# HGRN2 within-chunk products: one 64-wide block as two 32-wide ones, and another order of the small products

## The chip, the cores and the metric

The kernel runs on one core of a Trainium2 chip. A run is told by its device time in microseconds. The kernel before was run three times: 2319.0, 2328.68 and 2331.19 us, median 2328.68 us. Its profile is of one more execution, of 2322.79 us.

TensorE (PE in the profile) multiplies; VectorE (DVE), ScalarE (ACT) and GpSimd (POOL) work element by element; SyncE (SP) issues the DMAs.

## The reference, cut to what matters

One layer with two branches: a gated DeltaNet and an HGRN2 recurrence, over 256 context tokens and 2048 latent tokens in both directions. The change lies in the HGRN2 branch. With k = 1 - f and g = log f, the state of one head obeys

```python
# S_t = diag(f_t) S_{t-1} + k_t v_t^T ,  o_t = S_t^T q_t ; 4 heads, dk = dv = 128
qg, kg = q * exp(G), k * exp(-G)          # G: running sum of g in a chunk
attn = where(incl, einsum('bhncd,bhnsd->bhncs', qg, kg), 0.0)
o_c = einsum('bhcd,bhdv->bhcv', qg_c, S) + einsum('bhcs,bhsv->bhcv', attn_c, v_c)
S = S * gl_c[..., None] + einsum('bhcd,bhcv->bhdv', kd_c, v_c)
```

`attn` is a lower triangle (an upper one for the reversed direction): token c sees token s only from its own past. All arrays are float32.

## The kernel before, in words

The tokens are projected first, then comes the HGRN2 stage (lines 483 to 674), then the DeltaNet stages, then the merge of the branches. In the HGRN2 stage the kernel takes chunks of 128 tokens, four chunks (index `i`) to a scan group of 512 tokens. `scan_group(h, d, g, ps, S)` does one group of head `h` and direction `d`; latent groups (`lat`) are those with outputs: 4 heads, 2 directions and 4 groups make 32 of them. A group has these steps: ACT and DVE turn the projected gate into decays (lines 502 to 561), DVE and POOL make the scaled copies `ag`, `bg`, `a64`, `b64`, `b32`, PE transposes (L577) and forms the state update `pS` (L582), PE forms the triangle `pat`, DVE copies its valid part to `atB` (L604), and PE adds the state's part and the triangle's part into `pw` (L612, L613) while DVE carries the state on (L618).

The triangle of one 128-token chunk is built of blocks, because the decays of far tokens need a scale of their own: four diagonal blocks of 32 by 32 (the loop before line 600), then two blocks of 32 by 32 that join the 32-token blocks in pairs, and one of 64 by 64 that joins the two halves. All contract over the 128 partitions. `mm` (L591) issues each of them: L593 in direction 0, L595 in direction 1. Where its output lies in `pat` decides which 32-column strips of the PE array hold its weights: an output on partitions 32k to 32k+31 uses strip k, the 64 by 64 block uses strips 0 and 1 (direction 0) or 2 and 3 (direction 1). The two joining blocks of 32 use strips 0 and 2 (direction 0) or 1 and 3 (direction 1). The four diagonal blocks use strips 0, 1, 2, 3. A float32 product is two passes on PE, each with a weight load (LDWEIGHTS, on the line PEld) and a MATMUL.

`proj` (L205 to L207), called by `head_units` and `gate_block`, fills PE between the groups' steps with full-width products of the next head. What stands in which order on PE is not the order of the source: `TileContext(nc, schedule_with_timeline_sim=True)` (L1184) has a planner at build time that simulates the engines and puts the instructions of each engine into one fixed order. So full-width products (L577, L582, L612, L613, L205 to L207) can stand between two products of one group's triangle.

Of the kernel before, what the change touches and what calls it, by code (L numbers as in the profile page):

```python
# [39 lines left out]
def block_kernel(ctx, tc, x, c, ctx_in, c_ctx, w_mod, b_mod, w_in, conv_w, a_log, dt_bias,  # L40
# [436 lines left out]
    with tc.tile_pool(name="rb", reuse_waits="tile", bufs=1, side="right") as rb, \  # L477
# [12 lines left out]
        def bl(a):  # L490
            return slice(32 * a, 32 * a + 32)

        def b4(t):
            return t.rearrange("p c (b t) -> p c b t", t=32)

        def scan_group(h, d, g, ps, S):
# [56 lines left out]
            a = X.rearrange("p (c t) -> p c t", t=P)  # L553
# [9 lines left out]
            def fb(f, m):  # L563
                return f.unsqueeze(3).to_broadcast([P, k_, m, 32])
# [18 lines left out]
            if lat:  # L583
                a64 = rb.tile([P, 4, 64], F32, tag="a64", name="a64")
                b64 = rb.tile([P, 4, 64], F32, tag="b64", name="b64")
                b32 = rb.tile([P, 4, 64], F32, tag="b32", name="b32")
                ve.tensor_tensor(out=b4(a64), in0=b4(a)[:, :, 2:4], in1=fb(f2, 2), op=ALU.mult)
                po.tensor_tensor(out=b4(b64), in0=b4(b)[:, :, 0:2], in1=fb(f3, 2), op=ALU.mult)
                po.tensor_tensor(out=b4(b32), in0=b4(b)[:, :, 0:4:2], in1=fb(f4, 2), op=ALU.mult)

                def mm(i, am, bm, asl, bsl):  # L591
                    if d == 0:
                        te.matmul(out=pat[bsl, i, asl], lhsT=bm, rhs=am, start=True, stop=True)  # L593
                    else:
                        te.matmul(out=pat[asl, i, bsl], lhsT=am, rhs=bm, start=True, stop=True)  # L595

                for i in range(4):
                    for k in range(4):
                        mm(i, a[:, i, bl(k)], b[:, i, bl(k)], bl(k), bl(k))
                for i in range(4):  # L600
                    for k in range(2):
                        mm(i, a[:, i, bl(2 * k + 1)], b32[:, i, bl(k)], bl(2 * k + 1), bl(2 * k))
                    mm(i, a64[:, i, :], b64[:, i, :], slice(64, 128), slice(0, 64))
                ve.copy_predicated(out=atB[d], mask=mk[d].unsqueeze(1).to_broadcast([P, 4, P]), data=pat)  # L604
                o = rb.tile([P, 4, P], F32, tag="o", name="o")
                if d == 1:
                    sy.dma_start(out=o, in_=oP[h, g])
                pw = pb.tile([P, 4, P], F32, tag="o", name="pw")
                qg = ag if d == 0 else bg
# [54 lines left out]
        for h in range(H):  # L664
            fill = head_units(h + 1) if h + 1 < H else gate_units(NEARLY + GA)
            for d in range(2):
                w = load_w((C_FF, C_FB)[d] + h * P)
                S = None
                for j, g in enumerate(((4, 0, 1, 2, 3), (4, 3, 2, 1, 0))[d]):
                    S = scan_group(h, d, g, proj(w, g), S)  # L670
                    for _ in range(FBI[d][j] if h + 1 < H else FB[j] * d):
                        next(fill, None)
            for _ in fill:
                pass
# [514 lines left out]
```

## Time and profile before

| | us |
|---|---|
| runs before, median (lowest to highest) | 2328.68 (2319.0 to 2331.19) |
| the profiled execution | 2322.79 |
| its span in the trace | 2321.1 |
| PE busy | 2210.0 (95%) |
| DVE busy | 1401.9 (60%) |
| ACT busy | 907.8 (39%) |
| POOL busy | 756.9 (33%) |

The span runs from the first to the last instruction of the program; 1.7 us of the execution lie around it. Busy time is the time in which an engine has at least one instruction in work; PE's instructions overlap, so that one that the profile shows as 0.2 us long may start a few nanoseconds behind the one ahead of it. The mean granted clock of PE was 0.982 of full speed. The HGRN2 triangle's products run between 524.8 and 1060.6 us.

### The profile page before, as it was taken

The page shows a single profiled execution, that of the slowest core. Times are in us where ns is not written, and L with a number is a line of the kernel's source. Part 1 is how long each engine was busy: PE and PEld are TensorE (multiplying, and loading weights), DVE is VectorE, ACT ScalarE, POOL GpSimd, SP SyncE. Part 2 cuts the span into 40 slices and gives each one's busy share as a digit, 9 for nine tenths or more (in the row PEclk, how much of TensorE's full clock was granted, in tenths as well). Part 3 has the DMA queues.
Part 4 walks back from the last instruction along what each step waited for, and adds up shares of the span by engine and source line. Part 5 has one row for each costly group of instructions (what it writes and reads, how often), then busy time and mean ns, then how long its engine had stood idle before and what let it go on. Part 6 is the DMA issues. An engine that isn't in the chain of part 4 may idle for free. (4 is left out here: it accounts for less than half of the span.)

```text
span 2321.1 us, 39923 instructions
## 1 busy us (share of the span) xinstructions
PE 2210.0 (95%) x14998; PEld 1848.3 (80%) x14998; DVE 1401.9 (60%) x3184; ACT 907.8 (39%) x2298; POOL 756.9 (33%) x736
## 2 busy tenths in 40 slices
PE   7899999999999999999989999999989889999998
PEld 2778888888888888888878778788878878878887
DVE  5926666636766667774374877872332358566655
ACT  3523222234343444432434445544544454344321
POOL 3613343302221122224534445311133234334341
PEclk8999999999999999999999999999999999999999
DMA  8312222322322322224656588786887855434322
GB/s 317 112 36 73 66 73 71 87 63 78 92 71 85 91 74 87 85 76 132 178 163 195 185 243 256 206 240 204 250 271 264 264 192 166 127 110 128 118 82 78
DMA packets 298329, 330.24 MB, mean 142 GB/s; under 512 B 77536, under 2 KB 216918, under 8 KB 298136
## 3 DMA queue, kind: packets, MB, share of 16 engines
q1 hardware_dynamic: 298135, 327.69, 45.9%
q8 instruction: 118, 1.93, 0.4%
q14 instruction: 76, 0.61, 0.1%
HBM read 216.83 MB, written 110.79 MB: 141 GB/s over the span
## 5 line engine op out<-in xcount | busy, mean ns | idle before, releaser
L205 PE MATMUL ps<-uhi,wh 128*128 128x512 f32 (+1 forms) x1824 | 707.9, 388 | 5.4 <-DVE uhi L293 2.6
L206 PE MATMUL ps<-ulo,wh 128*128 128x512 f32 (+1 forms) x1824 | 705.8, 387 | 3.0 <-DVE ulo L295 2.7
L207 PE MATMUL ps<-uhi,wl 128*128 128x512 f32 (+1 forms) x1824 | 706.2, 387 | 0.5 <-POOL wl L197 0.5
L205 PEld LDWEIGHTS ps<-uhi,wh 128*128 128x128 f32 x1824 | 345.6, 190 | 71.0 <-DVE uhi L293 3.9
L206 PEld LDWEIGHTS ps<-ulo,wh 128*128 128x128 f32 x1824 | 345.7, 190 | 66.8 <-DVE ulo L295 3.9
L207 PEld LDWEIGHTS ps<-uhi,wl 128*128 128x128 f32 x1824 | 345.2, 189 | 64.5 <-POOL wl L197 1.3
L197 POOL TENSOR_TENSOR wl<-ws,wh 128x512 fp32r<-128x512 f32 x144 | 192.2, 1335 | 536.7 <-ACT wh L196 512.3
L196 ACT CAST wh<-ws 128x512 fp32r<-128x512 f32 x144 | 89.5, 621 | 288.5 <-DMA ws<-in_w_in_dram 192.3
L1089 PE MATMUL py<-yh,wab 128*128 128x256 f32 x512 | 151.4, 296 | 26.5 <-DVE mg L1092 25.6
L393 DVE SCALAR_TENSOR_TENSOR acc<-raw,cols,acc 128x512 f32<-128x512 f32 x192 | 153.9, 855 | 0.8
L1090 PE MATMUL py<-yl,wab 128*128 128x256 f32 x512 | 148.3, 290 | 2.6 <-POOL yl L1073 2.6
L1091 PE MATMUL py<-yh,wab 128*128 128x256 f32 x512 | 147.9, 289 | 0.0
L1089 PEld LDWEIGHTS py<-yh,wab 128*128 128x128 f32 x512 | 100.7, 197 | 31.0 <-DVE mg L1092 29.0
L572 POOL TENSOR_TENSOR bg<-s,fz 128x512 f32<-128x512 f32 (+1 forms) x36 | 38.0, 1057 | 263.5 <-ACT X L552 96.9
L1109 PE MATMUL pso<-uhi,mh 128*128 128x512 f32 x256 | 102.9, 404 | 3.6 <-ACT mh L1095 2.3
L1090 PEld LDWEIGHTS py<-yl,wab 128*128 128x128 f32 x512 | 101.0, 197 | 3.8 <-POOL yl L1073 3.2
L1111 PE MATMUL pso<-uhi,ml 128*128 128x512 f32 x256 | 102.0, 404 | 2.0 <-DVE ml L1096 1.9
L1110 PE MATMUL pso<-ulo,mh 128*128 128x512 f32 x256 | 101.6, 399 | 0.0
L1091 PEld LDWEIGHTS py<-yh,wab 128*128 128x128 f32 x512 | 101.2, 198 | 0.0
L1073 POOL TENSOR_TENSOR yl<-gt,yh 128x512 fp32r<-128x512 f32 x32 | 46.7, 1478 | 165.2 <-ACT yh L1072 165.2
L1096 DVE TENSOR_TENSOR ml<-mg,mh 128x256 fp32r<-128x256 f32 x64 | 53.0, 832 | 70.1 <-ACT mh L1095 69.4
L1095 ACT CAST mh<-mg 128x256 fp32r<-128x256 f32 x64 | 41.2, 651 | 135.7 <-DVE mg L1093 135.4
(371 smaller groups left out, 4135.8 us busy)
## 6 DMA issues: line engine op xcount, KB each, us to landing
ws<-in_w_in_dram SPq DMA_DIRECT2D x144, 256.0 KB, 3.2
gT<-gt SPq DMA_DIRECT2D x96, 256.0 KB, 3.2
kv<-knvD SPq DMA_DIRECT2D x36, 512.0 KB, 5.4
kq<-qkvD SPq DMA_DIRECT2D x32, 512.0 KB, 5.5
an<-atN SPq DMA_DIRECT2D x32, 512.0 KB, 5.7
mg<-gT SPq DMA_DIRECT2D x64, 256.0 KB, 3.6
qkvD<-acc SPq DMA_DIRECT2D x48, 256.0 KB, 2.3
l<-qkvD SPq DMA_DIRECT2D x16, 768.0 KB, 5.1
```

The lines of the kernel that those rows point to most:

```text
L196: ac.copy(out=wh[:, j:j + 4, :], in_=ws)
L197: po.tensor_tensor(out=wl[:, j:j + 4, :], in0=ws, in1=wh[:, j:j + 4, :].bitcast(F32), op=ALU.subtract)
L205: te.matmul(out=ps, lhsT=wh[:, k, :], rhs=uhi[gi][:, k, :], start=(k == 0), stop=False)
L206: te.matmul(out=ps, lhsT=wh[:, k, :], rhs=ulo[gi][:, k, :], start=False, stop=False)
L207: te.matmul(out=ps, lhsT=wl[:, k, :], rhs=uhi[gi][:, k, :], start=False, stop=(k == KB - 1))
L393: ve.scalar_tensor_tensor(out=a_, in0=raw[:, o + k:o + k + n], scalar=wk, in1=a_, op0=ALU.mult, op1=ALU.add)
L1089: te.matmul(out=py[:, i, :], lhsT=wh[:, k, ms_], rhs=yh[i][:, k, :], start=(k == 0), stop=False)
L1090: te.matmul(out=py[:, i, :], lhsT=wh[:, k, ms_], rhs=yl[i][:, k, :], start=False, stop=False)
L1091: te.matmul(out=py[:, i, :], lhsT=wl[:, k, ms_], rhs=yh[i][:, k, :], start=False, stop=(k == H - 1))
L1109: te.matmul(out=ps, lhsT=mh[:, k, ts_], rhs=wout[0][k][:, ns], start=(k == 0), stop=False)
L1110: te.matmul(out=ps, lhsT=mh[:, k, ts_], rhs=wout[1][k][:, ns], start=False, stop=False)
L1111: te.matmul(out=ps, lhsT=ml[:, k, ts_], rhs=wout[0][k][:, ns], start=False, stop=(k == KB - 1))
```

## The change

The 64 by 64 block of each chunk becomes two products of 32 weight columns and 64 streamed columns: in direction 0 the weights are 32 columns of `b64` and all of `a64` is streamed, in direction 1 the weights are 32 columns of `a64` and all of `b64` is streamed. The same numbers land on the same partitions of `pat`. In each chunk the four products are issued with the strips 0, 2, 0, 1 in direction 0 and 3, 1, 3, 2 in direction 1, where it was strips 0, 2, (0 and 1) and 1, 3, (2 and 3). The diagonal blocks are as before.

```diff
+                def across32(i, k):
+                    mm(i, a[:, i, bl(2 * k + 1)], b32[:, i, bl(k)], bl(2 * k + 1), bl(2 * k))
+
+                def across64(i, k):
+                    if d == 0:
+                        mm(i, a64[:, i, :], b64[:, i, bl(k)], slice(64, 128), bl(k))
+                    else:
+                        mm(i, a64[:, i, bl(k)], b64[:, i, :], bl(2 + k), slice(0, 64))
+
                 for i in range(4):
                     for k in range(4):
                         mm(i, a[:, i, bl(k)], b[:, i, bl(k)], bl(k), bl(k))
                 for i in range(4):
-                    for k in range(2):
-                        mm(i, a[:, i, bl(2 * k + 1)], b32[:, i, bl(k)], bl(2 * k + 1), bl(2 * k))
-                    mm(i, a64[:, i, :], b64[:, i, :], slice(64, 128), slice(0, 64))
+                    across32(i, d)
+                    across32(i, 1 - d)
+                    across64(i, d)
+                    across64(i, 1 - d)
```

## Rows read from the trace of the kernel before

**Rows 1.** The page: busy time by engine, and the PE line of 40 slices.
```profile
PE 2210.0 (95%) x14998; PEld 1848.3 (80%) x14998; DVE 1401.9 (60%) x3184; ACT 907.8 (39%) x2298; POOL 756.9 (33%) x736
...
PE   7899999999999999999989999999989889999998
```
**Rows 2.** Windows: start:end, length, each engine's busy time, clock, DMA.
```profile
520.00:1065.00 545.00, 544.01 (x4402) 455.40 (x4401) 383.96 (x1046) 219.11 (x400) 126.67 (x129) 1.00 0.28 83
520.00:965.00 445.00, 444.62 (x3504) 373.63 (x3503) 306.62 (x835) 179.88 (x328) 99.57 (x102) 1.00 0.28 83
965.00:1018.00 53.00, 53.00 (x475) 44.11 (x473) 45.14 (x129) 23.53 (x44) 13.36 (x15) 1.00 0.25 73
```
**Rows 3.** Waits of PE, 520 to 1065 us: total us, times, longest.
```profile
PE pS L582 <- DMA v<-vB: 0.6, 1, 0.6
PE pw L612 <- DVE S L618: 0.4, 1, 0.4
```
**Rows 4.** Timeline of PE, one group's joining blocks: start, us to last end, count.
```profile
526.25 0.26 PE L593 MATMUL pat<-X,b 128*32 128x32 f32 x4
526.44 0.33 PE L593 MATMUL pat<-a,b 128*64 128x64 f32 x2
526.70 0.26 PE L593 MATMUL pat<-X,b 128*32 128x32 f32 x4
...
527.77 0.33 PE L593 MATMUL pat<-a,b 128*64 128x64 f32 x2
528.02 0.49 PE L612 MATMUL pw<-S,ag 128*128 128x128 f32 x2
```
**Rows 5.** Timeline of PE, diagonal blocks on four strips, two stretches.
```profile
524.83 0.33 PE L593 MATMUL pat<-X,s 128*32 128x32 f32 x16
...
591.27 0.41 PE L595 MATMUL pat<-s,X 128*32 128x32 f32 x26
591.50 0.20 PE L595 MATMUL pat<-b,X 128*32 128x32 f32 x1
591.51 0.20 PE L595 MATMUL pat<-s,X 128*32 128x32 f32 x2
591.53 0.25 PE L595 MATMUL pat<-b,X 128*32 128x32 f32 x3
591.71 0.33 PE L595 MATMUL pat<-b,a 128*64 128x64 f32 x2
```
**Rows 6.** Tile pat: count, ns of one (min/median/max), first and last start.
```profile
L593 PE MATMUL pat<-X,b x256: 196/196/217, 526.3 to 1001.0; 128*32 128x32 f32 x128
L593 PE MATMUL pat<-a,b x128: 222/246/271, 526.4 to 1001.2; 128*64 128x64 f32 x128
L595 PE MATMUL pat<-b,X x256: 196/196/217, 591.5 to 1060.3; 128*32 128x32 f32 x128
L595 PE MATMUL pat<-b,a x128: 222/246/270, 591.7 to 1060.6; 128*64 128x64 f32 x128
```
**Rows 7.** Timeline of PE, joining blocks with full-width products among them.
```profile
548.34 0.33 PE L593 MATMUL pat<-a,b 128*64 128x64 f32 x2
548.60 0.49 PE L612 MATMUL pw<-S,ag 128*128 128x128 f32 x2
548.92 0.39 PE L613 MATMUL pw<-v,atB 128*128 128x128 f32 x2
549.24 0.26 PE L593 MATMUL pat<-X,b 128*32 128x32 f32 x4
...
1058.48 0.33 PE L595 MATMUL pat<-b,a 128*64 128x64 f32 x2
...
1060.01 0.33 PE L595 MATMUL pat<-b,a 128*64 128x64 f32 x2
...
1060.45 0.33 PE L595 MATMUL pat<-b,a 128*64 128x64 f32 x2
```
**Rows 8.** Waits of DVE, 520 to 1065 us: total us, times, longest.
```profile
DVE atB L604 <- PE pat L595: 31.8, 9, 4.9
```
**Rows 9.** Groups by line and shape: count, busy us, mean ns of one, idle before.
```profile
L613 PE MATMUL pw<-v,atB 128*128 128x128 f32 x256 | 49.5, 275 | 0.0
```

## The prediction, made blind

> **What bounds the kernel now.** I read the page first: PE is busy 95% of the span, and in no slice under seven tenths [rows 1]. Then the windows over the stretch in which the changed products run, 520 to 1065 us: PE is busy for 544.0 of 545 us, DVE for 384.0, ACT for 219.1, POOL for 126.7, the DMAs have 28%, and the clock is granted whole [rows 2]. Then PE's own waits there: 0.6 and 0.4 us, and nothing else [rows 3]. So in this stage PE's sequence is the time: a nanosecond taken out of it comes off the end, until some other engine is late. The chain that ended last shows only the end of the kernel and says nothing here.
>
> Being busy isn't the same as being used well. The timeline of one group's joining blocks shows the cost [rows 4]: four passes of the 32-wide blocks open at 526.25, the two passes of the 64-wide one at 526.44, the next 32-wide ones at 526.70, and the fourth turn ends where the full-width L612 opens, at 528.02. That is 1.77 us for four turns, 443 ns a turn, for eight array passes that stream 32 or 64 columns.
>
> **The prices.** In the diagonal blocks, on four strips in rotation, 16 passes end 0.33 us after the first began and 26 passes 0.41 us [rows 5]: ten passes more in 0.08 us, 8 ns a pass, so 32 ns a pass on any one of four strips. I take 31 to 32. A pass is 196 ns long in the records at 32 streamed columns and 222 at 64 [rows 6]; the 26 ns between them are 32 columns more, so a 64-column pass occupies a strip for about 57 ns if nothing else holds it.
>
> Between strips there is no pause: in the second stretch of rows 5 a joining product (`b,X`) starts at 591.50, before the last two diagonal passes (`s,X`) at 591.51. The strips go their own way, past each other in program order. Between widths there is one. In rows 4 the last of four 32-wide passes starts 0.26 - 0.196 = 0.06 us after the first, at 526.31, and the 64-wide one opens at 526.44: 0.13 us later, where 32-wide ones follow in 8 to 32 ns. Its second pass starts 0.33 - 0.222 = 0.11 us on, at 526.55, and the next 32-wide one at 526.70: 0.15 us. Of that a 64-column pass itself takes 53 (twice 26), a 32-column one 26, so both ways about 0.1 us passes with the array empty. Each 64-wide block costs two such pauses, or about 200 of the 443 ns.
>
> **The change part by part.** (1) The 64-wide form goes: 256 passes, 128 products [rows 6]. In their place stand 256 products of 32 weight columns and 64 streamed ones, 512 passes, so MATMUL and LDWEIGHTS grow by 256 each, to 15254 [rows 1].
>
> (2) All products of a triangle now have one width, so the pauses inside it go. The new turn, in direction 0, is strip 0 with 32 columns, strip 2 with 32, strip 0 with 64, strip 1 with 64; in direction 1 it is 3, 1, 3, 2. The fullest strip has 2 x 31 + 2 x 57 = 176 ns of passes, the others 114 and 62, beside it. From below a turn takes 176 ns. From above, if a strip's second product must wait for the whole turn ahead of it and nothing runs beside anything: 4 x 31 + 4 x 57 = 352 ns. In between, if the two products ahead must end before the two behind start: about 234 (62 + 114 and two fillings of about 29). I take 176, because rows 5 show the strips passing each other, and a strip that never runs dry sets the pace.
>
> (3) The number of turns. Followed along the timeline, of 128 64-wide blocks 87 are followed by another 32-wide product (the first at 526.44, the last at 1058.48), 39 by a full-width product (527.77 the first, 1060.45 the last), and two more have a full-width one ahead of them (one at 1060.01) [rows 4, 7]. That is 32 group ends and some places where the planner put a full-width product in. For the 87: 443 - 176 = 267 ns each, 23.2 us. For the 39 the pause to full width stays: first product 0 to about 53 ns with its weight load, then 31 + 57, and 152 to the full-width product, 293 ns for 443, so 150 ns each, 5.8 us. The two I count like the 39: 0.3 us. Sum: 29.3 us, in 32 groups 0.9 us each.
>
> The same counts with a turn of 234: 18.2 + 5.8 - 2.3 (the pair takes 58 ns longer in the 39 as well) = about 21.7 us. With 352: 87 x 91 = 7.9, nothing at the 39 (352 - 57 + 152 = 447), 8 us.
>
> (4) What else moves. No wait is new: the same copies `a64`, `b64`, `b32` feed the same products, and the order within a turn asks for none sooner than before. No DMA, no buffer, no DVE instruction is added. The copy to `atB` waits for PE, not PE for it: DVE stood 31.8 us in nine such waits [rows 8], and it moves up with PE.
>
> (5) What is late next. A group that is 0.9 us shorter on PE meets producers that aren't. PE waited 0.4 us for the state on DVE once [rows 3]; were that so in each of 32 groups, 13 us would be lost, from below none. DVE has 30% to spare over the stage, but it is 85% busy from 965 to 1018 us, where four groups stand close [rows 2]: 11.3 of 13.25 us a group, so 0.9 us less leaves it room there too. Rows 3 stand nearer to the lower end; I take 5 us.
>
> 29.3 - 5 = 24 us. From the profiled execution's 2322.8 us that is 2298.5; that execution lies 5.9 us under the median of the runs, within their 2319 to 2331. I name 2300.
>
> **A rule against the change.** The diagonal blocks' 16 passes in 0.33 us [rows 5] have the same 128 rows of the array, and one starts about 8 ns behind another. The Trainium skill ("TensorE: Matmul & The Clock Gate", Part 3: Packing small matmuls) says that a weight load overlaps matmuls in flight only when their row groups differ. By that rule these passes would stand one behind another, load and stream in turn; the trace disagrees for strips that differ. Another page of the Trainium skill ("TensorEngine Tiling (Array Packing)", Instruction Overhead) gives each matmul some 60 cycles and advises against tiling a dimension that is small already; at 2.4 GHz eight passes would by that estimate take 200 ns a turn, and the sum would be some 2.5 us smaller.
>
> **The rivals.**
> A, same strip in line (chance 0.07): strips 0 and 3 are used twice in a turn, and no row shows one strip twice with a single product between. If the second use holds up all that stands behind it, a turn is 352 ns, the gain 8 us, and the time 2315. For it: the rotation is not a clean one. Against: a strip's two passes already follow one another without holding up the next strip [rows 5].
>
> B, the other engines take half (0.18): PE waits where it now doesn't: in each group about as long as the one wait of rows 3, 0.45 us or half of its 0.9. The gain is 14 us, the time 2309. For it: POOL's and DVE's copies end shortly ahead of PE's products, the state's chain already let PE wait [rows 3]. Against: DVE's 30%.
>
> C, slower, the planner breaks the triangle up (0.10): the order on PE is set at build by a planner, and each full-width stretch that it puts between two 32-wide products costs two pauses. Price from rows 7: the 64-wide block's second pass starts at 548.45, then come four full-width passes, and the next 32-wide one starts at 549.24, 0.79 us on; 26 ns of it are the wider pass's own. Elsewhere such a pass costs 0.39 - 0.275 = 0.115 us [rows 7, 9], four of them 0.46 us, and the 32-wide product would have come anyway within 0.03: so some 0.27 us each time. 29 us are eaten by 108 more such places, three or four in each group. It decides from there: with 150 more the time is 2334. For it: the planner gets more places to do so, and has done it within the joining blocks seven times. Against: full-width products there only shift, and most groups have an unbroken joining loop [rows 4]. More than half of this chance ends slower, the rest within 0.5%.
>
> D, slower, one pass at a time (0.03): no overlap at all, load and stream in turn. A lone strip's second pass starts 53 ns behind its first (the four passes of rows 4 start within 0.06 us, two strips 7 ns apart), a 64-column one 79: 4 x 53 + 4 x 79 = 528 ns a turn, 85 ns more for the 87 and 158 more for the 39, 13.6 us in all, 2336. This is what the rule on row groups, quoted above from the Trainium skill, would do. Rows 5 speak against it.
>
> **How the numbers follow.** The forecast has 0.62, and its own range is 2288 to 2308: 29 us with nothing lost and 5 us of spread downwards, 21.7 less half the loss upwards. To leave out no more than 2 in 10 the range takes in B and most of A: 2287 to 2320. A measurement tells about 0.5% from no change, 11.6 us of 2328.7. Faster: the forecast and nearly all of B, 0.79. Same: A, the rest of B and part of C, 0.14. Slower: D and the larger part of C, 0.07.
>
> **What would show it.** Right: the form 128*64 is gone from tile pat, with 512 passes of 128*32 streaming 64 columns; an unbroken joining loop takes 0.85 to 0.95 us from its first pass to the next full-width product, not 1.77; the last triangle product, at 1060.6 us now, comes about 24 us sooner; PE's waits from 520 us on stay under some 6 us. Step 2 is wrong if four turns take more than 1.1 us; step 5 if PE's idle time in the stage exceeds 10 us; step 3 if the count of stretches of full-width products inside the triangles rises much. The stages behind 1060 us should be as long as before; if they aren't, the planner moved more than this stage.

## The result, and the profile after

The changed kernel takes 2307.02 us (median of five runs, 2303.73 to 2311.25) where the kernel before, in the same comparison, takes 2328.65: a ratio of 0.9917 with a 95% interval from 0.9898 to 0.9936. By the ratio that is 19.3 us off, between 14.9 and 23.8 (the two medians alone would give 21.6); the forecast had 24 off the profiled execution and named 2300.

Read first whether the stage in question moved as said. The head of the page after, with PE's busy time and counts:

```profile
span 2305.3 us, 40427 instructions
...
PE 2195.9 (95%) x15254; PEld 1845.4 (80%) x15254; DVE 1402.9 (61%) x3184; ACT 908.0 (39%) x2298; POOL 765.1 (33%) x736
```

MATMUL and LDWEIGHTS stand at 15254, 256 more than in rows 1. PE's timeline over the joining blocks of the group of rows 4 (start, us to the last end, count):

```profile
525.19 0.22 PE L593 MATMUL pat<-X,b 128*32 128x32 f32 x2
525.21 0.24 PE L593 MATMUL pat<-a,b 128*32 128x64 f32 x1
525.25 0.20 PE L593 MATMUL pat<-X,b 128*32 128x32 f32 x2
...
525.39 0.19 PE L593 MATMUL pat<-X,b 128*32 128x32 f32 x1
...
525.57 0.19 PE L593 MATMUL pat<-X,b 128*32 128x32 f32 x1
...
525.74 0.19 PE L593 MATMUL pat<-X,b 128*32 128x32 f32 x1
...
525.80 0.28 PE L593 MATMUL pat<-a,b 128*32 128x64 f32 x3
526.01 0.49 PE L623 MATMUL pw<-S,ag 128*128 128x128 f32 x2
```

From 525.19 to the full-width L623 at 526.01 are 0.82 us, where rows 4 have 1.77. The rows at 525.39, 525.57 and 525.74 recur with the turn: 0.17 to 0.18 us. A 64-column pass of `a,b` starts 0.02 us behind the first `X,b` instead of 0.19.

The last triangle product, in the tile's rows (count, ns of one, first and last start), with the first one of the stage:

```profile
L593 PE MATMUL pat<-X,s x512: 196/196/263, 523.8 to 976.6; 128*32 128x32 f32 x171
...
L595 PE MATMUL pat<-b,a x256: 219/219/243, 586.2 to 1035.6; 128*32 128x64 f32 x128
```

From first to last start the triangle stage is 511.8 us long; before it was 535.8 (524.8 in rows 5 to 1060.6 in rows 6): 24.0 us less. PE's waits over 520 to 1065 us, to be held against rows 3:

```profile
PE pw L623 <- DVE S L629: 1.9, 3, 0.9
PE pw L623 <- DVE ag L569: 0.9, 2, 0.5
PE pS L582 <- DMA v<-vB: 0.7, 1, 0.7
PE pw L623 <- DVE fz L535: 0.5, 1, 0.5
PE pk L577 <- POOL bg L572: 0.5, 2, 0.3
```

They are 4.5 us instead of 1.0. So the stage gave what it should, and part of it came back behind it: 2321.1 - 1060.6 = 1260.5 us before, 2305.3 - 1035.6 = 1269.7 after, 9.2 us more for work that the change does not touch. Both numbers are of one execution each, and the one of the kernel before was a quick one, 5.9 us under its median. By the ratio of the timed runs less came back: the stage is 24.0 us shorter and starts 1.0 sooner, and 19.3 were left, so some 6 us.

The windows from the last triangle product on, before and then after: to the first transposes of the DeltaNet preparation, to the end of its last levels, to the first merge product, to the end. The columns are those of rows 2, the third from the end the granted clock. The levels are the small products into the tile `lvt`.

```profile
1061.00:1085.00 24.00, 24.00 (x121) 20.27 (x121) 4.80 (x9) 1.98 (x4) 8.19 (x10) 1.00 0.45 132
1085.00:1684.00 599.00, 572.28 (x4654) 478.38 (x4652) 365.31 (x1015) 282.68 (x927) 224.98 (x271) 0.99 0.70 209
1684.00:1884.00 200.00, 180.05 (x1123) 160.15 (x1122) 63.36 (x180) 87.84 (x288) 59.23 (x47) 0.97 0.79 259
1884.00:2321.00 437.00, 393.93 (x2415) 348.94 (x2414) 276.72 (x422) 157.38 (x419) 160.72 (x94) 0.96 0.38 120
```

```profile
1036.00:1059.00 23.00, 23.00 (x114) 19.39 (x114) 4.40 (x9) 1.83 (x4) 9.58 (x12) 1.00 0.42 126
1059.00:1674.00 615.00, 586.36 (x4655) 492.12 (x4653) 366.21 (x1015) 282.38 (x927) 221.88 (x268) 0.96 0.68 204
1674.00:1871.00 197.00, 180.56 (x1123) 160.80 (x1123) 63.32 (x177) 87.77 (x288) 59.21 (x47) 0.97 0.79 263
1871.00:2305.00 434.00, 394.90 (x2416) 350.70 (x2415) 277.03 (x422) 157.41 (x419) 162.07 (x94) 0.96 0.38 121
```

The same 4650 or so matmuls stand in the second stretch of both, and it takes 615 us for 599, at a mean clock of 0.96 for 0.99. The other three stretches are 7 us shorter together. What differs in the second one, besides the clock, is the order: followed along the two traces, the products on PE and the instructions on DVE and ACT stand in another sequence, from the HGRN2 stage on.

### The profile page after: what moved, and what is told of

Read it like the earlier page. It is cut to its first block, busy times and chain, and to the rows that moved or that the text cites. A ratio compares the mean times of both kernels' runs of the same rounds, so it can differ in the third digit from the quotient of the medians.

```text
span 2305.3 us, 40427 instructions
## 1 busy us (share of the span) xinstructions
PE 2195.9 (95%) x15254; PEld 1845.4 (80%) x15254; DVE 1402.9 (61%) x3184; ACT 908.0 (39%) x2298; POOL 765.1 (33%) x736
## 5 line engine op out<-in xcount | busy, mean ns | idle before, releaser
L205 PE MATMUL ps<-uhi,wh 128*128 128x512 f32 (+1 forms) x1824 | 707.1, 388 | 6.7 <-DVE gt L220 4.0
L207 PE MATMUL ps<-uhi,wl 128*128 128x512 f32 (+1 forms) x1824 | 705.8, 387 | 0.5 <-POOL wl L197 0.5
L205 PEld LDWEIGHTS ps<-uhi,wh 128*128 128x128 f32 x1824 | 345.8, 190 | 73.7 <-DVE gt L220 5.0
L207 PEld LDWEIGHTS ps<-uhi,wl 128*128 128x128 f32 x1824 | 345.9, 190 | 63.8 <-POOL wl L197 0.9
L197 POOL TENSOR_TENSOR wl<-ws,wh 128x512 fp32r<-128x512 f32 x144 | 197.9, 1374 | 535.1 <-ACT wh L196 516.1
```

What stands on the lines that cost most here:

```text
L197: po.tensor_tensor(out=wl[:, j:j + 4, :], in0=ws, in1=wh[:, j:j + 4, :].bitcast(F32), op=ALU.subtract)
L205: te.matmul(out=ps, lhsT=wh[:, k, :], rhs=uhi[gi][:, k, :], start=(k == 0), stop=False)
L207: te.matmul(out=ps, lhsT=wl[:, k, :], rhs=uhi[gi][:, k, :], start=False, stop=(k == KB - 1))
```

## The experiments

Each was timed beside the kernel before, and its ratio is to that. Stages and stretches are read from one profiled execution each.

**split_only.** The split without the new order of blocks.

```diff
-                    across32(i, d)
-                    across32(i, 1 - d)
-                    across64(i, d)
-                    across64(i, 1 - d)
+                    across32(i, 0)
+                    across32(i, 1)
+                    across64(i, 0)
+                    across64(i, 1)
```

> The 64-wide block is split as in the changed kernel, but the four products of a turn stand in the old order of blocks in both directions (strips 0, 2, 0, 1 and 1, 3, 2, 3). The planner gives every engine the same sequence of forms as in the changed kernel. My theory, that the gain is the width switches and that the order within a turn is worth nothing because the fullest strip (176 ns a turn) sets the pace: the unbroken joining loop takes 0.82 us as in the changed kernel, the time is within 0.2% of 2307. Rival, the rotation carries part of it: the loops of direction 1 get longer by up to 57 ns a turn, 0.2 us a group of 16, 3 to 4 us in all. On what was given back behind the triangle stage (1260 us from the last triangle product to the end before, 1269.5 after): if the planner's sequence makes it, the same 1267 to 1272 comes here, with 45 to 60 us of half clock between 1036 and 1700 us; if it is chance of the run, it falls anywhere from 1258 to 1272.

Measured: 2308.17 us, ratio 0.9920 (0.9897 to 0.9942). A joining loop of direction 1, the first and last triangle product, and the second stretch behind them:

```profile
585.31 0.20 PE L595 MATMUL pat<-b,X 128*32 128x32 f32 x1
...
586.12 0.49 PE L623 MATMUL pw<-S,bg 128*128 128x128 f32 x2
```
```profile
L593 PE MATMUL pat<-X,s x512: 196/196/218, 523.1 to 975.2; 128*32 128x32 f32 x171
...
L595 PE MATMUL pat<-b,a x256: 219/219/243, 585.3 to 1035.4; 128*32 128x64 f32 x128
```
```profile
1059.00:1678.00 619.00, 585.90 (x4652) 492.02 (x4650) 365.84 (x1015) 282.66 (x927) 221.61 (x268) 0.96 0.68 203
```

The loop takes 0.81 us and the stage 512.3, where the changed kernel has 0.82 and 511.8. The rival's 0.2 us a group isn't there, so the new order of the blocks within a turn is worth nothing here: the whole effect in the stage is the split. PE's products stand in the same sequence as in the changed kernel. Behind it the stretch takes 1271.5 us (2306.9 - 1035.4) with the clock at 0.96 again: what came back is there again with the same sequence.

**order_only.** The block whole, its two companions swapped in direction 1.

```diff
-                    for k in range(2):
+                    for k in (d, 1 - d):
```

> The 64 by 64 block stays whole; in direction 1 its two companions swap places (strips 3, 1, then 2 and 3). The planner's sequence of forms is that of the kernel before. Theory: nothing changes, a turn stays 443 ns, the time is within 0.3% of the kernel before; from the last triangle product to the end it takes 1260 us give or take 3, with 15 to 20 us of half clock between 1061 and 1700. Rival, the order matters by itself: direction 1 gets faster by up to 30 ns a turn, 2 us in all. If what was given back is chance of the run, the stretch behind the triangle stage differs from 1260 by up to 10 us here.

Measured: 2329.57 us, ratio 1.0009 (0.9994 to 1.0025); no change. Its last triangle product and its second stretch:

```profile
L595 PE MATMUL pat<-b,a x128: 222/246/270, 592.5 to 1061.4; 128*64 128x64 f32 x128
```
```profile
1086.00:1691.00 605.00, 577.12 (x4652) 482.93 (x4651) 368.75 (x1015) 282.91 (x927) 224.48 (x271) 0.98 0.69 207
```

The stage is 535.8 us long as before (525.6 to 1061.4), so the rival's 2 us aren't there. The second stretch is 6 us longer than in the kernel before with the same sequence, so a few microseconds of it do change from run to run, with the clock. All behind the triangle stage, from 1061.4 to 2323.4, takes 1262.0 us for 1260.5.

**grouped64.** No split: the two widths one after the other.

```diff
                     for k in range(2):
                         mm(i, a[:, i, bl(2 * k + 1)], b32[:, i, bl(k)], bl(2 * k + 1), bl(2 * k))
+                for i in range(4):
                     mm(i, a64[:, i, :], b64[:, i, :], slice(64, 128), slice(0, 64))
```

> No split: first all eight 32-wide joining products of a group, then its four 64-wide ones, so two width switches instead of eight. Theory, the switches are what was paid: an unbroken joining loop takes 8 products on two strips 0.25 us, a switch 0.13, eight 64-wide passes some 54 ns apart 0.38, the way out 0.15, so 0.9 us instead of 1.77 and of 0.82 after the change; the triangle stage is 20 to 24 us shorter than before. Rival, a 64-wide pass is slow by itself and not by the switch: the loop stays at 1.6 us or more and the stage loses under 5 us. The planner will order the rest anew; the stretch behind the triangle stage can take from 1255 to 1275 us.

Measured: 2301.59 us, ratio 0.9890 (0.9866 to 0.9914). The joining blocks of the same group, PE's timeline:

```profile
526.91 0.45 PE L593 MATMUL pat<-X,b 128*32 128x32 f32 x16
527.29 0.68 PE L593 MATMUL pat<-a,b 128*64 128x64 f32 x8
527.90 0.49 PE L613 MATMUL pw<-S,ag 128*128 128x128 f32 x2
```
```profile
L593 PE MATMUL pat<-X,s x512: 196/196/217, 525.5 to 978.9; 128*32 128x32 f32 x171
...
L595 PE MATMUL pat<-b,a x128: 222/222/270, 587.7 to 1037.6; 128*64 128x64 f32 x128
```

0.99 us a group, against 1.77 and 0.82, with not one product more than before. With nothing between them, eight 64-wide passes take 0.61 us from the first start to the next product's start. The stage runs from 525.5 to 1037.6, 512.1 us: 23.7 less than before. So a 64-wide pass is not slow by itself: the pause between widths is what was paid, and avoiding it by order does nearly as much as avoiding it by the split. The planner's sequence for it is a third one, and behind the stage it takes 1261.5 us, where the changed kernel takes 1269.7: in the profiles its time is the lower one for that. The intervals of the two ratios overlap.

**by_strip.** The split products strip by strip, which takes the rotation away.

```diff
-                for i in range(4):
-                    across32(i, d)
-                    across32(i, 1 - d)
-                    across64(i, d)
-                    across64(i, 1 - d)
+                for prods in (((across32, 0), (across64, 0)), ((across64, 1),), ((across32, 1),)) if d == 0 else \
+                        (((across32, 1), (across64, 1)), ((across64, 0),), ((across32, 0),)):
+                    for i in range(4):
+                        for f, k in prods:
+                            f(i, k)
```

> Split as in the changed kernel, but the products stand strip by strip: first all eight of the fullest strip over the four chunks, then the four of one, then the four of the other. Theory one, PE looks far enough ahead to run a strip's products beside those of another wherever they stand: the joining loop stays at 0.82 us. Theory two, it looks ahead only a few products, so the rotation is needed: the loop takes up to 0.70 + 0.46 + 0.25 = 1.4 us and the triangle stage is 10 to 18 us longer than in the changed kernel.

Measured: 2317.96 us, ratio 0.9961 (0.9947 to 0.9976). Its joining blocks:

```profile
525.01 0.25 PE L593 MATMUL pat<-X,b 128*32 128x32 f32 x2
...
525.62 0.41 PE L593 MATMUL pat<-a,b 128*32 128x64 f32 x6
525.82 0.22 PE L593 MATMUL pat<-X,b 128*32 128x32 f32 x1
525.87 0.22 PE L593 MATMUL pat<-a,b 128*32 128x64 f32 x1
...
525.92 0.22 PE L593 MATMUL pat<-a,b 128*32 128x64 f32 x1
...
525.98 0.22 PE L593 MATMUL pat<-a,b 128*32 128x64 f32 x1
...
526.19 0.49 PE L623 MATMUL pw<-S,ag 128*128 128x128 f32 x2
```
```profile
L593 PE MATMUL pat<-X,s x512: 196/196/218, 523.6 to 982.4; 128*32 128x32 f32 x171
...
L595 PE MATMUL pat<-b,X x256: 192/196/217, 587.0 to 1043.6; 128*32 128x32 f32 x128
```

1.18 us a group, between the two theories' 0.82 and 1.4: the last strip's `X,b` start only at 525.82, when the products ahead are nearly through. PE starts some products past a busy strip, but here it didn't go past the whole set that stood ahead. The stage takes 520.0 us (523.6 to 1043.6), 8 more than with the products mixed, less than the 10 to 18 of theory two. So some rotation is needed, and the old order of blocks (split_only) has enough of it already.

**new_products_old_sequence and old_products_new_sequence.** Two kernels that part the products from the planner's sequence. When the program is built, each engine's instructions are bound to a given sequence by edges that fix only the order of issue. The sequence is that of the kernel before or that of the changed one, and a split block's second half follows its first. In the code, `order` holds one engine's instructions as they were planned in the other kernel (cut to the lines that bind them). The traces bear it out: PE's products stand in the intended sequence in both.

```diff
+        for x, y in zip(order, order[1:]):
+            tc.add_manual_dep(y, x.name, info, reason="plan")
```

> The products of the changed kernel (64-wide block split, order of blocks as in split_only, which ran like the changed kernel), but every engine's sequence is pinned to that of the kernel before, each second half of a split block right behind its first. Theory: the 9 to 11 us that come back behind the triangle stage are the price of the planner's new sequence, not of the products. Then the triangle stage takes 512 to 514 us as in the changed kernel, the stretch behind it 1258 to 1263 us as in the kernel before (half clock from the first transposes to the last levels 13 to 25 us, not 50), and the time is 2298 to 2303. Rival, they come back because that stage starts 25 us sooner or because of the chip's own clock: 1269 to 1272 behind, the time 2307 to 2310.

Measured: 2300.9 us, ratio 0.9886 (0.9865 to 0.9907). Its first and last triangle products, and its second stretch:

```profile
L595 PE MATMUL pat<-X,s x512: 196/196/218, 525.2 to 977.2; 128*32 128x32 f32 x171
...
L597 PE MATMUL pat<-b,a x256: 219/219/243, 589.0 to 1035.7; 128*32 128x64 f32 x128
```
```profile
1061.00:1667.00 606.00, 577.94 (x4650) 483.93 (x4649) 363.98 (x1015) 283.82 (x928) 223.85 (x271) 0.98 0.69 207
```

> The products of the kernel before (64-wide block whole), but every engine's sequence is pinned to that of the changed kernel. Theory, the sequence costs by itself: the triangle stage takes 534 to 540 us with the width switches in it, the stretch behind it 1269 to 1272 us with 40 to 55 us of half clock from the first transposes to the last levels, and the time is 2331 to 2338, slower than before. Rival, the sequence costs nothing: 1260 behind, the time that of the kernel before, 2322 to 2330.

Measured: 2335.6 us, ratio 1.0033 (1.0017 to 1.0048), slower than before.

```profile
L593 PE MATMUL pat<-X,s x512: 196/196/218, 523.7 to 999.4; 128*32 128x32 f32 x171
...
L595 PE MATMUL pat<-b,a x128: 222/246/270, 588.6 to 1061.8; 128*64 128x64 f32 x128
```
```profile
1086.00:1705.00 619.00, 590.10 (x4655) 494.53 (x4653) 368.56 (x1015) 282.85 (x927) 222.00 (x268) 0.95 0.68 203
```

With the two kernels that they were made from they fill a square (a time or ratios to the kernel before; the stage and what is behind it in us):

| | old sequence | new sequence |
|---|---|---|
| old products | 2328.65 us; stage 535.8, behind 1260.5 | 1.0033; stage 538.1, behind 1272.3 |
| new products | 0.9886; stage 510.5, behind 1264.7 | 0.9917; stage 511.8, behind 1269.7 |

Read down, the products save 25 or 26 us in the stage in either sequence. Read across, the new sequence costs behind it 11.8 us with the old products and 5.0 with the new ones; the quick execution in the first cell makes the one large, and the timed runs have 0.0033 and 0.0031 of the time, 7 to 8 us. With the old products that is clear of noise; with the new ones the two intervals still overlap. With the new products in the old sequence the stage is 1.5 us shorter than I expected and the stretch behind it, 1264.7, 1.7 us longer; the rival's 1269 to 1272 and 2307 to 2310 are refuted.

**tail_work6 and tail_work2.** Is the lower clock the price of the sequence? The fill, full-width products L205 to L207 that the planner puts between the small ones, runs out in the changed kernel at 1621 us, and the levels of the last chunks stand without it to 1674 us, at a clock of 0.78. Call that the tail. Here the levels of the last five chunks got extra full-width products (18 or 6 a chunk, into columns that are overwritten), in the pinned sequence of the changed kernel. The code shown is tail_work6's; tail_work2 has `range(2)`. `idle_work()` is called behind the first, second and third set of products of `levels()`.

```diff
+            def idle_work():
+                if pos >= 13:
+                    for k in range(6):
+                        EXTRA.append(te.matmul(out=lvt[:, :, 64:128], lhsT=uhi[2][:, k, 0:P], rhs=uhi[2][:, k, 0:256],
+                                               start=True, stop=True).ins.name)
```

> The changed kernel's products and its sequence (pinned, as in split_only), and in the levels of the last five chunks, where the full-width fill has run out, PE gets 18 extra full-width products of 256 columns a chunk, whose results are overwritten: some 90 of them, 10 us at 2.4 GHz, put behind products that are followed by waits. Theory, the loss behind the triangle stage is half clock in that tail (27 to 31 us of it between 1630 and 1690 us in the changed kernel and split_only): the extra work keeps the clock up, half clock in the tail falls under 10 us and gives back some 9 us, so in spite of 10 us more work the levels end no more than 3 us later than in split_only and the time is 2303 to 2311. Rival, the tail is bound by DVE, ACT and DMAs and the clock is only a sign of it: the clock comes up as well, but the added work comes on top, 5 to 10 us, and the time is 2313 or more; or the clock stays low and 20 us are added.

> As tail_work6 with 6 extra products a chunk instead of 18: some 30, 3 us at 2.4 GHz. Theory: half clock in the tail falls by a part, and the time is 2302 to 2309, at most that of split_only. Rival: 2309 to 2312.

Measured: 2311.88 us, ratio 0.9934 (0.9911 to 0.9956), and 2312.03, 0.9936 (0.9914 to 0.9959). The window from about the end of the fill to the end of the levels, in split_only, in tail_work6 and in tail_work2:

```profile
1624.00:1679.00 55.00, 50.31 (x581) 45.28 (x575) 21.14 (x67) 24.41 (x86) 5.97 (x14) 0.74 0.70 202
```
```profile
1621.00:1677.00 56.00, 50.18 (x673) 45.16 (x673) 21.22 (x68) 26.45 (x93) 6.02 (x14) 1.00 0.68 200
```
```profile
1625.00:1676.00 51.00, 45.30 (x615) 40.65 (x614) 20.72 (x67) 25.34 (x89) 6.03 (x14) 0.93 0.73 216
```

With all of the extra work the clock came up from 0.74 to 1.00, and about 90 more matmuls were done in 56 us where there were 55. With a third of it the clock came up to 0.93, and the tail is 4 us shorter. So in the tail it went as the theory has it: the levels end 2 us earlier in tail_work6 than in split_only (last product at 1676.6 and 1678.2), where the theory allowed 3 later and the rival had 5 to 10 on top. The time as a whole gained nothing: both kernels lie above what I expected, the first by 0.9 us and the second by 3; the first is under the rival's bound and the second at the upper end of its range. In the profiles the loss stands behind the levels, where nothing was changed: from the last product of the levels to the end it is 628.7 us in split_only (1678.2 to 2306.9), 636.7 in tail_work6 (1676.6 to 2313.3) and 635.2 in tail_work2 (1675.1 to 2310.3). In the kernel before that stretch is 637.3 (1683.8 to 2321.1), so it moves by as much from one execution to another, and single executions don't say whether the extra work did it. That a chain of waits sets a part of the tail stays open: in split_only PE was idle there for 5 of 55 us, which could have taken up a part of the added work.

## Why the prediction was right, and where it was not

The time lies in the range, 7 us above the one named, with the sign and nearly the size forecast. Most of the 7 us are the base: the 24 us were taken off a quick execution, and off the median of 2328.65 they would have given 2304.7. The range's own upper bound, 2308, doesn't come out of the terms named for it: 21.7 less half the loss of 5 off 2322.8 is 2303.6.

**The bound and the prices.** That the stage is PE's sequence and nothing else held: with the old sequence the stage is 25.3 us shorter (535.8 to 510.5) while PE's waits there rose by 4.3 us, from 1.0 to 5.3. That makes 29.6 us of pauses and passes taken out, where the sum said 29.3. The turn of 176 ns was 0.17 to 0.18 us, the loop 0.82 us where 0.85 to 0.95 was named. The turn of 234 ns rested on fillings of 29 ns that no run shows; nothing like it came. The pause between widths, taken from the two starts in rows 4, is confirmed by grouped64, which only removes switches.

**The loss to other engines.** 5 us were set down; the waits rose by 3.5 us in the changed kernel. So 27.5 us were taken out there (24.0 and 3.5), not 29.3, and the two misses cancel: that the stage gave 24.0 us to the tenth is luck. The largest part, 1.9 of 4.5 us, is where rows 3 pointed, the state on DVE for L623. Rival B, half the gain, is out.

**Rival A**, one strip twice with a single product between, is refuted for the order used (the turn is the fullest strip's own passes); by_strip, with eight products of one strip in line, shows that strips do hold each other up when the line is long. **Rival D** is out: passes that all use the same 128 rows start 0.02 us apart on different strips (525.19 and 525.21). The Trainium skill's rule on row groups ("TensorE: Matmul & The Clock Gate", Part 3: Packing small matmuls) doesn't hold for these column strips: by it they would stand in turn.

**Rival C**, the planner, named the right agent and the wrong place. I asked what it would do inside the triangles, and it did little there: counted along the traces, a joining loop is left for a full-width product 48 times before and 43 times after. The step that failed is the silent term of the sum: that all behind 1060 us stays as long as before. It became 9.2 us longer in the profiles, some 6 by the timed runs, and the square shows why: with four products in a turn instead of three the planner gave another sequence for the rest of the program, and that sequence costs 0.3%, shown with the old products and alike in size, though not clear of noise, with the new ones. The forecast had only the sign of how to see it ("the planner moved more than this stage"), no price.

**What that sequence costs by, in part open.** Over the kernels above the stretch of the preparation and levels takes 599 us at a clock of 0.99, 604 to 606 at 0.98, 615 to 619 at 0.96 and 619 at 0.95. The granted clock has two levels, 1.2 and 2.4 GHz, so a mean that falls from 0.99 to 0.96 over 615 us says that 0.03 x 2 x 615 = 37 us more were spent at the lower one; at half the pace that loses 18 us at most, and 16 were lost.

In the changed kernel's tail the clock fell after the fill had run out at 1621 us, with 53 us of small products still to come; before, the fill lasted until 1638, 46 us from the end of the levels. The tail also shows the clock and the length moving together where the instructions and their sequence are the same, in the kernel before and in order_only:

```profile
1638.00:1684.00 46.00, 41.73 (x629) 36.83 (x627) 20.71 (x68) 26.34 (x92) 5.98 (x14) 1.00 0.77 239
```
```profile
1641.00:1691.00 50.00, 45.76 (x626) 40.67 (x625) 21.21 (x68) 26.49 (x92) 5.97 (x14) 0.90 0.73 220
```

4 us more at a clock lower by 0.10 over 50 us, which is 10 us at the lower level and 5 us of loss at most. In new_products_old_sequence the same tail takes 51 us at 0.90. The timed runs agree: of the 48 runs of the kernel before beside the experiments the six shortest (2319 to 2322 us) have a mean clock of 0.980 to 0.982, the six longest (2333 to 2336) 0.975 to 0.978. As an estimate, time times clock takes the loss out: it is 2280 us for the kernel before and 2278 for its products in the new sequence, 2251 for the changed kernel and 2256 for the new products in the old sequence. So the products are worth 24 to 27 us by it, and the sequence costs no more than the clock accounts for.

That the lower clock and the longer stretch go together is shown, also where the instructions and their order are the same. That it is the cause of the whole price is not: raising the clock shortened the tail of tail_work2, but not the time.

**A version that is as good or better.** The new products in the old sequence (2300.9 us) and the grouped 64-wide blocks (2301.6 us) both lie under the changed kernel's 2307.0, by 0.3%; their intervals still overlap with its own.

## What to carry to other kernels

When PE is busy all the time, look at what is between the passes: a change of the products' width cost 0.1 us each way here, more than a pass itself, and either splitting to one width or grouping by width gets it back. Small products on different column strips ran beside each other here, at 8 ns a pass on four strips, when neighbours in the order used different strips; exact rotation wasn't needed. And where a planner orders the program, a change in the number or the order of instructions can also change the order of everything behind it: measure the two apart by pinning the sequence before judging the change by its total. Hold a profiled execution against the median of the runs before taking a difference from it.

## What the runs showed of the hardware that was not expected

In by_strip PE did start products past a busy strip, but the third strip's only 0.81 us after the first strip's (525.01 and 525.82): so how far it looks ahead is limited. When it did start them, three passes of the products ahead hadn't begun; how far it can look is not shown beyond that. And a dense set of 64-wide float32 products is not slow: eight passes in 0.61 us, some 76 ns each with the pause behind them counted, where one pair alone between narrower products took 0.26 us from its start to the next product [rows 4].
